# A decoder block's output projection: which heads it takes first, and where the attention's last pieces are put in place

## The chip, the cores and the metric

The kernel runs on one core of a Trainium2 chip. What counts is the device time of one execution in microseconds; the times below are medians of several executions. The core has a matrix engine (TensorE, PE in the profile, with PEld for its weight loads), a vector engine (VectorE, DVE), an activation engine (ScalarE, ACT), a general engine (GpSimd, POOL) and a queue engine (SyncE, SP), which here only issues DMAs. ACT and POOL also issue DMAs.

## The reference, cut to what matters

```python
def token_mixer(h, ...):                       # h: [1, 512, 2048]
    proj = h @ w_in
    ...
    o_a = gla_chunked(...)                     # linear attention, 4 heads of 256 columns
    gate = jax.nn.silu(gg)                     # gg: 1024 columns of proj
    o_a = (rmsnorm(o_a, gla_norm) * gate).reshape(B, S, GLA_V)
    ...
    o_b = diff_attention(dq, dk, dv, lam)      # softmax attention, 4 heads of 256 columns
    o_b = (rmsnorm(o_b, diff_norm) * (1.0 - lambda_init)).reshape(B, S, DIFF_V)
    o = jnp.concatenate([o_a, o_b], axis=-1)   # [1, 512, 2048]
    return o @ w_o                             # w_o: [2048, 2048]

x = x + rmsnorm(token_mixer(rmsnorm(x)), attn_post_norm)
x = x + rmsnorm(conv_ffn(rmsnorm(x)), ffn_post_norm)
```

Rows 0 to 1023 of `w_o` meet the linear attention's heads, rows 1024 to 2047 the softmax attention's. All is float32.

## The kernel before, in words

**Split products.** Every large product is done with each float32 operand split in two parts of a faster kind, `hi` and `lo`, and three matmuls (hi·hi, hi·lo, lo·hi). Activations stand in SBUF as `ah` and `al`, [128, 4 token blocks, 16 slots of 128 features, 128 tokens]. Weights come in tiles of 512 KB (`raw`, four buffers; `wt` for some) on the SP queue. `granule` (L128) splits one: ACT copies it to `hi` (L137), DVE subtracts to get `lo` (L138). The parts go to `ring`, which holds three tiles.

**Units.** The input projection is done mostly in ten units (`InUnit`, L696). A unit makes a 2 by 2 block product of tokens by columns with seven block products instead of eight, called x0, z0, y0, z1, x1, y1, y2. Each takes two weight tiles, 24 matmuls of 128x128 on 128x256 each (L742 to L748). The operands are `ah`/`al` itself or sums of its blocks: x0 reads block a11 (tokens 0 to 255, slots 0 to 7), x1 reads a12 (the same tokens, slots 8 to 15), y1 reads s7, which was written over tokens 256 to 511, slots 0 to 7, and y2 reads a22 (tokens 256 to 511, slots 8 to 15). y1 and y2 use weight tiles to which POOL's DMAs have added another block (`more`, L720). The last two units, `gate_unit(0)` and `gate_unit(1)`, make the gate of the linear attention. Each of their four results is multiplied with a head's output loaded from DRAM (`op`), passed through a sigmoid and multiplied again (L819 to L821). The first unit's results go to DRAM (`ogd`); the second's are kept in SBUF (`kept_u`).

**Attention beside them.** The two attentions are generators in the list `fill`, the linear one first. `step()` is called after each weight tile and moves them on by `pace[0]` steps, 0.75 for most of the projection; `drain()` runs what is left. The softmax attention (`diff_heads`, L586) has 16 pieces of work (4 heads by 4 query blocks) in a pipeline of 21 steps: scores and softmax, transposes two steps later (L637), the product with the values another step later (L646) with its square sum on ACT (L649), its root on POOL (L144, L146) and the scaling on DVE (L652), and two steps later the transposes of the result (L659), a copy (L661) and a store to DRAM from ACT (`dstd`, L662). Each step of the generator is program order for all engines.

**Putting in place.** Two helpers bring the mixer's result into `ah` and `al`, whose old contents the units have then done with. `place_diff(i)` does the softmax attention: for each head it loads tokens 256 i to 256 i + 255 from `dstd` (`dt`, 256 KB, on SP) and splits them into slots 0 to 7, on ACT (L150) and DVE (L151). `turn_gate(i)` does the gated linear attention for the same tokens: it loads `ogt` from `ogd` (256 KB, on SP), transposes that and the kept blocks on PE (L833) and splits them into slots 8 to 15 with the same two lines. `dt` and `ogt` share the four buffers of the tag `qk` with the attention's queries and keys.

**Output projection.** `proj_n` (L196) makes 512 columns at a time: for each weight tile (two slots of 128 rows) and each of four token blocks six matmuls of 128x128 on 128x512 (L191 to L193) into four PSUM banks. It takes three column blocks; the fourth is in `to_ffn`, which goes on into the next norm and the feed-forward part and whose order on the engines is written out by hand (`manual_schedule`). Before the change the weight rows come as 1024 to 2047, then 0 to 1023, against slots 0 to 15.

**What sets the order.** Outside the hand-ordered blocks a planner orders each engine's instructions at build time, by program order and by when its own timing model says that inputs and buffers are there. At run time each engine's queue keeps that order, and each instruction waits for its inputs.

The end of the mixer, for the last unit, reads before the change: `u.y0()`, `u.z1()`, `drain()`, `place_diff(0)`, `u.x1()`, `turn_gate(0)`, `u.y1()`, `place_diff(1)`, `u.y2()`, `turn_gate(1)`.

Of the kernel before, what the change touches and what calls it, by code (L numbers as in the profile page):

```python
# [21 lines left out]
KT = D // P  # L22
# [13 lines left out]
def hybrid_layer(ctx: ExitStack, tc: tile.TileContext, x, attn_pre_norm, w_in, w_alpha_up, b_alpha,  # L36
# [6 lines left out]
    w_o3 = w_o[0].rearrange("(k p) c -> p k c", p=P)  # L43
# [37 lines left out]
    pace = [0.0, 0.0]  # L81
# [13 lines left out]
    def drain():  # L95
        while fill:
            for _ in fill.pop(0):
                pass

    def load(src, a, by=None):  # L100
        raw = wpool.tile([P, GR], F32, name="raw", tag="raw", bufs=4)
        (by or nc.sync).dma_start(out=raw.rearrange("p (a b) -> p a b", a=a), in_=src)
        return raw
# [9 lines left out]
    def halves():  # L113
        slot[0] = (slot[0] + 1) % 3
        return [ring[:, RS * i + p:RS * i + p + GR] for i, p in zip((slot[0], slot[0] + 3), place_w[0])]
# [3 lines left out]
    def spare_halves(pool):  # L119
        if pool == "rt":  # L120
            return [rp.tile([P, GR], F32R, name=n, tag="rt", bufs=4) for n in ("xhi", "xlo")]
        if pool is True:
            if not kept:
                kept.extend(small_tile(n, F32R) for n in ("xhi", "xlo"))
            return kept
        return [pool.tile([P, GR], F32R, name=n, tag=n, bufs=4) for n in ("xhi", "xlo")]

    def granule(src, a, raw=None, spare=None, hl=None):  # L128
        if raw is None:
            raw = load(src, a)  # L130
        if hl is not None:
            hi, lo = hl[:, 0, :], hl[:, 1, :]
        elif spare:
            hi, lo = spare_halves(spare)
        else:
            hi, lo = halves()
        act(hi, raw, AF.Copy)  # L137
        tt(lo, raw, hi.bitcast(F32), ALU.subtract)  # L138
        r = "p (a b) -> p a b"
        return hi.rearrange(r, a=a), lo.rearrange(r, a=a)  # L140
# [43 lines left out]
                    emit(n, banks[n])  # L184
            step()

    def mm_n(banks, t, g, w):
        for k in range(2):
            s = 2 * g + k
            st, sp = s == 0, s == KT - 1  # L190
            mm(banks[t], ah[:, t, s, :], w[0][:, k, :], start=st, stop=False)  # L191
            mm(banks[t], ah[:, t, s, :], w[1][:, k, :], start=False, stop=False)  # L192
            mm(banks[t], al[:, t, s, :], w[0][:, k, :], start=False, stop=sp)  # L193


    def proj_n(w3, col, emit, order=tuple(range(KT)), first=0, banks=None):  # L196
        if banks is None:
            banks = [bank(psm) for _ in range(NT)]
        for g in range(first, KT // 2):
            w = granule(w3[:, order[2 * g]:order[2 * g] + 2, col:col + 512], 2)  # L200
            for t in range(NT):
                mm_n(banks, t, g, w)
                if g == KT // 2 - 1:
                    emit(t, banks[t])
            step()
# [96 lines left out]
    with tc.manual_schedule(engines=IN_ORDER):  # L302
        banks = first_half(0)

    HK = KT // 2
# [11 lines left out]
    sp = mixer.enter_context(tc.tile_pool(name="sums", bufs=1))  # L317
# [521 lines left out]
    def turn_gate(i):  # L839
        for j in range(2):  # L840
            u = qk_tile("ogt")
            dma(two(u), ogd[:, 2 * i:2 * i + 2, 256 * j:256 * (j + 1)])
            turn_block(0, j, i, u)
            turn_block(1, j, i, kept_u.pop((j, i)))

    def place_diff(i):
        for h in range(DH):
            u = qk_tile("dt")
            dma(two(u), dstd[h][:, :, 256 * i:256 * (i + 1)])
            split(*(v[:, 2 * i:2 * i + 2, 2 * h:2 * h + 2, :].rearrange("p t n c -> p n t c") for v in (ah, al)),  # L850
                  u.rearrange("p (n t c) -> p n t c", n=2, t=2))
# [41 lines left out]
    banks = [bank(psm) for _ in range(2)]  # L893
# [14 lines left out]
    for i, u in enumerate(units):  # L908
        u.y0()
        if i - 1 in after:  # L910
            there[after[i - 1][0]] = after[i - 1][1]
        u.z1()
        pace[0] = 0.75
        if i < len(units) - 1:
            u.x1()
            u.y1()
            units[i + 1].x0()
            u.y2()
            units[i + 1].z0()
        else:  # L920
            drain()
            place_diff(0)
            u.x1()
            turn_gate(0)
            u.y1()
            place_diff(1)
            u.y2()
            turn_gate(1)
    mixer.close()


    x1d = [dram.tile([P, D], F32, name=f"x1d{t}") for t in range(NT)]
    wo = ExitStack()
    wp = wo.enter_context(tc.tile_pool(name="wo", bufs=1))
    m = [wp.tile([P, D], F32, name=f"m{t}") for t in range(NT)]
    g1 = wp.tile([P, D], F32, name="g1")
    g2 = wp.tile([P, D], F32, name="g2")
# [4 lines left out]
    def evac_m(c, t, b):  # L942
        sl = slice(512 * c, 512 * (c + 1))
        act(m[t][:, sl], b, AF.Square, accum_out=ssm[t][:, c:c + 1])
        tt(m[t][:, sl], b, g1[:, sl], ALU.mult)

    order = [(s + 8) % 16 for s in range(KT)]
    for c in range(3):
        proj_n(w_o3, 512 * c, lambda t, b, c=c: evac_m(c, t, b), order)

    def to_ffn():
        banks = [bank(psm) for _ in range(NT)]
        w, wa, wb, xr, rs = {}, {}, {}, {}, {}

        def weights(g):
            w[g] = granule(w_o3[:, order[2 * g]:order[2 * g] + 2, 1536:2048], 2, spare=wp if g > 3 else None)

        def prods(t, *gs):  # L960
            for g in gs:
                mm_n(banks, t, g, w[g])

        def evac(t):
            xr[t] = wp.tile([P, D], F32, name="xr", tag="xr", bufs=2)
            dma(xr[t], x2[t * P:(t + 1) * P, :])
            evac_m(3, t, banks[t])
            ss = small.tile([P, 1], F32, name="ss", tag="ss")
            nc.vector.reduce_sum(ss, ssm[t], axis=AX.X)
            rs[t] = rsqrt_mean(ss, D)  # L970

        def residual(t):
            stt(m[t], m[t], rs[t], xr[t], ALU.mult, ALU.add)
            dma(x1d[t], m[t])

        def square(t):
            ss = small.tile([P, 1], F32, name="ss", tag="ss")
            act(xr[t], m[t], AF.Square, accum_out=ss)
            rs[t] = rsqrt_mean(ss, D)

        def scale(t):
            for i in range(4):
                sl = slice(512 * i, 512 * (i + 1))
                stt(xr[t][:, sl], m[t][:, sl], rs[t], g2[:, sl], ALU.mult, ALU.mult)

        def turn(t, *ps):
            for i in ps:
                transpose_into_act(xr[t][:, 512 * i:512 * (i + 1)], t, 4 * i, 4)

        def weights_f(d, c0, g, spare=None):  # L990
            place_w[0] = APART
            d[g] = granule(w_f3[:, 4 * g:4 * g + 4, c0:c0 + 256], 4, spare=spare)

        for g in (0, 1, 2, 4):
            weights(g)
        for t in range(NT):
            prods(t, 0)
        for g in (3, 5, 6, 7):
            weights(g)
        prods(0, 1, 2, 3, 4, 5, 6, 7)  # L1000
        evac(0)
        residual(0)
        square(0)
        scale(0)
        prods(1, 1, 2, 3, 4, 5, 6, 7)
        evac(1)
        turn(0, 0, 1)
        residual(1)
        turn(0, 2, 3)
        square(1)  # L1010
        scale(1)
        prods(2, 1, 2, 3, 4, 5, 6, 7)
        evac(2)
        turn(1, 0, 1)
        residual(2)
        turn(1, 2, 3)
        square(2)
        prods(3, 1, 2, 3, 4, 5, 6, 7)
        weights_f(wa, 0, 0)
        weights_f(wa, 0, 1)  # L1020
        scale(2)
        evac(3)
        weights_f(wa, 0, 2)
        ba = [bank(psm) for _ in range(2)]
        bb = [bank(psm) for _ in range(2)]
        mm_t(ba, 0, wa[0], 0, 2)
        residual(3)
        turn(2, 0, 1, 2, 3)
        square(3)
        weights_f(wa, 0, 3, wp)  # L1030
        mm_t(ba, 1, wa[1], 0, 2)
        mm_t(ba, 2, wa[2], 0, 2)
        scale(3)
        weights_f(wb, DFF, 0, wp)
        mm_t(ba, 3, wa[3], 0, 2)
        turn(3, 0, 1, 2, 3)
        weights_f(wb, DFF, 1, wp)
        weights_f(wb, DFF, 2, wp)
        for g in range(3):
            mm_t(bb, g, wb[g], 0, 2)  # L1040
        for g in range(4):
            mm_t(ba, g, wa[g], 2, 4)
        bb2 = [bank() for _ in range(2)]
        for g in range(3):
            mm_t(bb2, g, wb[g], 2, 4)
        weights_f(wb, DFF, 3)
        mm_t(bb, 3, wb[3], 0, 2)
        mm_t(bb2, 3, wb[3], 2, 4)
        return ba, list(zip(bb, bb2))
# [444 lines left out]
    order = change_over(ups[-1])  # L1494
# [9 lines left out]
    for i, u in enumerate(downs):  # L1504
# [4 lines left out]
        first = i % 2 == 0  # L1509
# [147 lines left out]
```

## Time and profile before

| what | us |
|---|---|
| median of 3 runs | 2103.01 |
| lowest and highest run | 2099.64, 2104.24 |
| the profiled execution, its span (first to last instruction) | 2104.4 |
| PE busy in that span | 2062.8 (98%) |
| DVE busy | 1507.9 (72%) |
| ACT busy | 1001.9 (48%) |
| POOL busy | 287.5 (14%) |
| mean granted clock of TensorE | 0.996 |

No time of the profiled execution is given beside its span. A busy PE is not PE at its best: matmuls are pipelined and the profile models their ends. In the rows below a line such as L659 is that line of the kernel, `bank<-ident,on` names what is written and read, and a bracket at the end says how long the engine was idle before and which instruction ended that. Times are from the start of the span.

### The profile page before, as it was taken

The numbers are of one execution on the slowest core, as the hardware profiler recorded it, in microseconds if no ns is written. First come the engines' busy times: TensorE is split into PE (matmuls) and PEld (weight loads), VectorE is DVE, ScalarE is ACT, GpSimd is POOL, SyncE is SP. The second block draws the span as 40 slices with busy tenths as digits, with TensorE's granted clock in tenths as the row PEclk, the third lists the DMA queues.
The fourth block names the chain that finished last, engine by engine and source line by source line (L and its number), as shares of the span: only waits on it lengthen the run. The fifth ranks groups of instructions, "written<-read, shape, count | busy, mean of one in ns | idle before, by whom it ended". The sixth has DMA issues, their size and how long they took to land.

```text
span 2104.4 us, 35571 instructions
## 1 busy us (share of the span) xinstructions
PE 2062.8 (98%) x14449; PEld 1903.4 (90%) x14449; DVE 1507.9 (72%) x1802; ACT 1001.9 (48%) x1306; POOL 287.5 (14%) x306
## 2 busy tenths in 40 slices
PE   7999999999989999999999999999999999999998
PEld 6699999999988889899999999999999878787786
DVE  5967777676752255986777767777777778888877
ACT  4544444455742233454554545455455554444443
POOL 0112222322200000011111011111111110110100
PEclk9999999999999999999999999999999999999999
DMA  5488887878875344447668577567676876776663
GB/s 210 118 185 179 191 197 176 178 176 198 196 193 175 100 150 161 140 103 196 150 147 196 140 162 190 135 163 175 164 160 179 239 208 168 192 189 159 171 169 140
DMA packets 280696, 358.60 MB, mean 170 GB/s; under 512 B 14592, under 2 KB 221876, under 8 KB 278612
## 3 DMA queue, kind: packets, MB, share of 16 engines
q1 hardware_dynamic: 191380, 259.85, 37.1%
q0 software_dynamic: 84800, 94.38, 29.6%
q8 instruction: 113, 1.85, 0.4%
q10 hardware_dynamic: 4352, 2.10, 0.3%
q14 instruction: 51, 0.42, 0.1%
HBM read 311.72 MB, written 44.56 MB: 169 GB/s over the span
## 4 chain that ended last, share of the span: by engine, by line
issue 37%; PE 29%; POOL 3%; DMA 2%; DVE 2%; ACT 1%; POOLq 0%; DVEq 0%; ACTq 0%; SPq 0%
PE bank L1248 4%; PE bank L1247 4%; PE bank L1246 4%; PE bank L191 3%; PE bank L192 3%; PE bank L193 3%; POOL raw L1194 1%; POOL rt L1194 1%; PE bank L1349 1%; PE bank L1350 1%; PE bank L1348 1%; PE bank L1553 1%; PE bank L1554 1%; PE bank L1552 1%; PE bank L175 1%
## 5 line engine op out<-in xcount | busy, mean ns | idle before, releaser
L138 DVE TENSOR_TENSOR ring<-raw,ring 128x1024 fp32r<-128x1024 f32 x315 | 383.1, 1221 | 280.8 <-ACT ring L137 276.5
L137 ACT ACTIVATE ring<-raw 128x1024 fp32r<-128x1024 f32 x315 | 333.3, 1060 | 516.4 <-PE bank L1247 119.7
L1248 PE MATMUL bank<-ah,ring 128*128 128x256 f32 x1280 | 353.4, 276 | 0.7 <-DVE ring L138 0.7
L1246 PE MATMUL bank<-ah,ring 128*128 128x256 f32 x1280 | 353.3, 276 | 0.0
L1247 PE MATMUL bank<-al,ring 128*128 128x256 f32 x1280 | 353.3, 276 | 0.0
L137 ACT ACTIVATE ring<-rt 128x1024 fp32r<-128x1024 f32 x221 | 233.2, 1060 | 247.3 <-PE bank L1247 146.1
L138 DVE TENSOR_TENSOR ring<-rt,ring 128x1024 fp32r<-128x1024 f32 x221 | 268.8, 1221 | 91.6 <-ACT ring L137 89.7
L1248 PEld LDWEIGHTS bank<-ah,ring 128*128 128x128 f32 x1280 | 240.3, 188 | 0.9 <-DVE ring L138 0.9
L1246 PEld LDWEIGHTS bank<-ah,ring 128*128 128x128 f32 x1280 | 240.3, 188 | 0.1
L1247 PEld LDWEIGHTS bank<-al,ring 128*128 128x128 f32 x1280 | 240.3, 188 | 0.1
L1349 PE MATMUL bank<-ring,ah 128*128 128x512 f32 x424 | 166.2, 392 | 6.3 <-DVE ring L138 6.3
L1350 PE MATMUL bank<-ring,al 128*128 128x512 f32 x424 | 165.1, 389 | 0.0
L1348 PE MATMUL bank<-ring,ah 128*128 128x512 f32 x424 | 158.6, 391 | 0.7 <-ACT ring L137 0.7
L192 PE MATMUL bank<-ring,ah 128*128 128x512 f32 x280 | 111.1, 398 | 0.8 <-DVE ring L138 0.8
L191 PE MATMUL bank<-ring,ah 128*128 128x512 f32 x280 | 110.5, 400 | 0.3 <-ACT ah L150 0.3
L193 PE MATMUL bank<-ring,al 128*128 128x512 f32 x280 | 110.0, 396 | 0.0
L1194 POOL DMA_DIRECT2D raw<-in_w_ffn_in_dram x40 | 51.2, 1309 | 397.2 <-DVE ring L138 397.2
L1349 PEld LDWEIGHTS bank<-ring,ah 128*128 128x128 f32 x424 | 79.6, 188 | 26.0 <-DVE ring L138 9.9
L1348 PEld LDWEIGHTS bank<-ring,ah 128*128 128x128 f32 x424 | 79.3, 188 | 19.8 <-ACT ring L137 3.2
L1194 POOL DMA_DIRECT2D rt<-in_w_ffn_in_dram x40 | 51.0, 1285 | 326.2 <-DVE ring L138 303.7
L1350 PEld LDWEIGHTS bank<-ring,al 128*128 128x128 f32 x424 | 79.6, 188 | 16.4
L746 PE MATMUL bank<-ring,ah 128*128 128x256 f32 x320 | 92.6, 289 | 0.0
(346 smaller groups left out, 5675.3 us busy)
## 6 DMA issues: line engine op xcount, KB each, us to landing
raw<-in_w_ffn_in_dram SPq DMA_DIRECT2D x96, 512.0 KB, 5.0
raw<-in_w_in_dram SPq DMA_DIRECT2D x56, 512.0 KB, 4.6
raw<-in_w_ffn_out_dram SPq DMA_DIRECT2D x48, 512.0 KB, 6.8
raw<-in_w_in_dram POOLq DMA_DIRECT2D x40, 512.0 KB, 7.2
rt<-in_w_ffn_in_dram SPq DMA_DIRECT2D x40, 512.0 KB, 5.9
rt<-in_w_ffn_in_dram POOLq DMA_DIRECT2D x40, 512.0 KB, 6.1
raw<-in_w_ffn_in_dram POOLq DMA_DIRECT2D x40, 512.0 KB, 6.8
raw<-in_w_o_dram SPq DMA_DIRECT2D x32, 512.0 KB, 3.9
```

Of the source, the lines that this page charges most:

```text
L137: act(hi, raw, AF.Copy)
L138: tt(lo, raw, hi.bitcast(F32), ALU.subtract)
L191: mm(banks[t], ah[:, t, s, :], w[0][:, k, :], start=st, stop=False)
L192: mm(banks[t], ah[:, t, s, :], w[1][:, k, :], start=False, stop=False)
L193: mm(banks[t], al[:, t, s, :], w[0][:, k, :], start=False, stop=sp)
L1194: nc.gpsimd.dma_start(out=raws[g].rearrange("p (a b) -> p a b", a=self.a), in_=self.block(0, j, g), accum_op=ALU.add)
L1246: mm(o, wh, sh[:, :, kk, :], start=start and kk == 0 and n == 0, stop=False, **NOW)
L1247: mm(o, wh, sl[:, :, kk, :], start=False, stop=False, **NOW)
L1248: mm(o, wl, sh[:, :, kk, :], start=False, stop=kk == HK - 1, **NOW)
L1348: mm(b[j], sh[:, o:o + P], w[0][:, q, :], start=start and st == 0, stop=False, **NOW)
L1349: mm(b[j], sh[:, o:o + P], w[1][:, q, :], start=False, stop=False, **NOW)
L1350: mm(b[j], sl[:, o:o + P], w[0][:, q, :], start=False, stop=st == 3, **NOW)
```

## The change

The linear attention's heads come first in the output projection: weight rows 0 to 1023 are taken first and meet slots 8 to 15. `proj_n` and `mm_n` get a list of slots in place of an order of weight rows. `place_diff(0)`, `place_diff(1)` and `drain()` move behind `turn_gate(1)`, and the pace for the last three block products is set to one attention step for each call. The pool of the output projection's tiles, which lies over the mixer's memory, is made with `reuse_waits="tile"`: each of its tiles waits only for what lay under it, not for the whole pool before it.

```diff
-    def mm_n(banks, t, g, w):
+    def mm_n(banks, t, g, w, slots=tuple(range(KT))):
         for k in range(2):
-            s = 2 * g + k
-            st, sp = s == 0, s == KT - 1
+            i = 2 * g + k
+            st, sp, s = i == 0, i == KT - 1, slots[i]
             mm(banks[t], ah[:, t, s, :], w[0][:, k, :], start=st, stop=False)
...
-    def proj_n(w3, col, emit, order=tuple(range(KT)), first=0, banks=None):
+    def proj_n(w3, col, emit, slots=tuple(range(KT)), first=0, banks=None):
...
-            w = granule(w3[:, order[2 * g]:order[2 * g] + 2, col:col + 512], 2)
+            w = granule(w3[:, 2 * g:2 * g + 2, col:col + 512], 2)
             for t in range(NT):
-                mm_n(banks, t, g, w)
+                mm_n(banks, t, g, w, slots)
...
         else:
-            drain()
-            place_diff(0)
+            pace[0] = 1.0
             u.x1()
             turn_gate(0)
             u.y1()
-            place_diff(1)
             u.y2()
             turn_gate(1)
+            drain()
+            place_diff(0)
+            place_diff(1)
     mixer.close()
...
-    wp = wo.enter_context(tc.tile_pool(name="wo", bufs=1))
+    wp = wo.enter_context(tc.tile_pool(name="wo", bufs=1, reuse_waits="tile"))
...
-    order = [(s + 8) % 16 for s in range(KT)]
+    slots = [(s + HK) % KT for s in range(KT)]
     for c in range(3):
-        proj_n(w_o3, 512 * c, lambda t, b, c=c: evac_m(c, t, b), order)
+        proj_n(w_o3, 512 * c, lambda t, b, c=c: evac_m(c, t, b), slots)
...
-            w[g] = granule(w_o3[:, order[2 * g]:order[2 * g] + 2, 1536:2048], 2, spare=wp if g > 3 else None)
+            w[g] = granule(w_o3[:, 2 * g:2 * g + 2, 1536:2048], 2, spare=wp if g > 3 else None)
...
-                mm_n(banks, t, g, w[g])
+                mm_n(banks, t, g, w[g], slots)
```

## The prediction

> **What bounds the kernel now.** I read the page's first part, then TensorE's busy time by stretches around the edit, then the stretch that stands out, engine by engine.
>
> ```profile
> span 2104.4 us, 35571 instructions
> ...
> PE 2062.8 (98%) x14449; PEld 1903.4 (90%) x14449; DVE 1507.9 (72%) x1802; ACT 1001.9 (48%) x1306; POOL 287.5 (14%) x306
> ```
>
> TensorE (PE) is busy for 98% of the span, so what moves the time is a hole on PE or a slower PE. All idle time together is 2104.4 - 2062.8 = 41.6 us, and what the edit can win lies in the part of it near the edit. By stretches (length, then busy time of PE, PEld, DVE, ACT, POOL, then granted clock, DMA share, GB/s):
>
> ```profile
> 540.00:550.00 10.00, 8.60 (x63) 7.98 (x62) 7.62 (x16) 7.46 (x15) 2.55 (x3) 1.00 0.76 217
> ...
> 580.00:590.00 10.00, 10.00 (x82) 9.79 (x81) 3.06 (x3) 3.09 (x4) 2.91 (x3) 1.00 1.20 221
> 590.00:600.00 10.00, 4.30 (x22) 4.13 (x22) 3.92 (x6) 3.87 (x8) 0.88 (x2) 0.76 1.10 344
> 600.00:610.00 10.00, 10.00 (x82) 10.00 (x82) 7.15 (x10) 5.64 (x8) 0.00 (x0) 0.90 0.55 165
> ...
> 630.00:640.00 10.00, 10.00 (x46) 8.28 (x45) 3.31 (x4) 2.12 (x2) 0.00 (x0) 1.00 0.99 372
> ```
>
> The stretch from 590 to 600 us has 22 matmuls where its neighbours have 82, and the clock falls to 0.76 and 0.90 in it and the next. That stretch is the last gate unit's z1 and x1, where the edit is. PE in order of time (start, length, instruction, idle time before it):
>
> ```profile
> 584.22 1.89 PE L646 MATMUL bank<-dvt,aT 128*128 128x256 f32 x8
> ...
> 590.07 0.28 PE L746 MATMUL bank<-ring,in_s3h 128*128 128x256 f32 x1
> 596.05 0.66 PE L659 MATMUL bank<-ident,on 128*128 128x128 f32 x2 [5.70 <-DVE on L652]
> ...
> 596.93 0.41 PE L746 MATMUL bank<-ring,in_s3h 128*128 128x256 f32 x1
> ...
> 601.63 0.41 PE L747 MATMUL bank<-ring,al 128*128 128x256 f32 x1
> ...
> 602.04 0.28 PE L746 MATMUL bank<-ring,ah 128*128 128x256 f32 x1
> 602.15 0.28 PE L747 MATMUL bank<-ring,al 128*128 128x256 f32 x1
> ```
>
> PE stands 5.70 us in front of the transposes of the last attention step's output (L659), in the middle of z1's products. The value product that feeds them (L646, four key blocks) began at 584.22 and is modelled to end at 586.1. Why the output came so late is on ScalarE (ACT):
>
> ```profile
> 593.34 0.63 ACT L150 ACTIVATE ah<-dt 128x512 fp32r<-128x512 f32 x1 [7.94 <-DMA dt<-dstd]
> 593.87 0.37 ACT L649 ACTIVATE jk<-bank 128x256 f32<-128x256 f32 x1
> ```
>
> ACT stood 7.94 us before the first half of a split of `dt`, the fourth of `place_diff(0)`, and the square of the last attention step (L649) was behind it. In the program that square comes before `place_diff`; the planner, which sets the order here, put it behind. The chain of waits says what the split waited for (start, length):
>
> ```profile
> 579.90 7.53 DMA dstd<-dst
> 587.48 5.83 DMA dt<-dstd
> ```
>
> A store of 128 KB to DRAM and its load back, 13.4 us, in the stretch where the DMA share is 1.20. So the chain is: store, reload, split on ACT, square, norm, transposes, with PE's z1 products queued behind the transposes.
>
> **The change, part by part.**
>
> *The drain and the pace.* `step()` is called twice in each block product. Counting calls from where the two generators start, with 0.75 of a step each, the 53 steps of the linear attention, and the attention's steps with their yields while a head is not there, step 18 falls on z0's second half of the last unit, step 19 on y0's first and step 20, the last, on y0's second; z1's second half finds the generator ended. So `drain()` had nothing to do, and `pace[0] = 1.0` paces nothing. Moving them costs and gains 0. The attention's instructions are issued where they were; "dealt out" does not happen.
>
> *`place_diff` behind everything.* Its 8 loads on the SP queue, 8 splits on ACT and 8 on DVE remain in number. In program order they move past x1, y1, y2 and both `turn_gate`s, and on SP past three `op` loads and four `ogt` loads. The SP queue now:
>
> ```profile
> 587.48 0.52 SPq L48 DMA_DIRECT2D dt<-dstd  x1
> 588.11 0.61 SPq L48 DMA_DIRECT2D op<-oad  x1
> 588.78 1.00 SPq L48 DMA_DIRECT2D ogt<-ogd  x2
> ...
> 591.59 0.38 SPq L102 DMA_DIRECT2D raw<-in_w_o_dram  x1
> ```
>
> The fourth `dt` held up `op`, `ogt` and the first weights of w_o behind it. With the move, `ogt` takes the four buffers of tag qk first, so no `dt` can be asked for before an `ogt` is transposed, after x1. ACT then has nothing to stand before when the last value product ends. From square to transposes took 596.05 - 593.87 = 2.2 us; from 586.1 that is 588.3, before PE comes to the place at 590.35. The wait of 5.70 us goes; for a slower norm or an earlier place of the transposes I leave 0.2 us.
>
> *The clock behind the hole.* From 596.93 to 601.63 lie 23 matmuls, 22 steps of 0.214 us, where 602.04 to 602.15 is 0.11 us: 22 x 0.10 = 2.2 us lost. The two clock figures say the same from the other side: half clock for 4.8 and 2.0 us, of which PE worked from 596.05 to 602.0; half of that is 3.0 us. I take 2.8 us, since the rows leave out the edges. [...] The rows of 540 to 550 show the other side: 1.4 us idle, clock 1.00. So a short hole costs only itself.
>
> *What comes late next.* PE reaches y1 and y2 8.5 us earlier. y1's weights are the slowest, added to in place by POOL's DMAs, and the loads that matter land so (median us last):
>
> ```profile
> raw<-in_w_o_dram SPq DMA_DIRECT2D x10, 512.0 KB, 4.2
> ...
> dt<-dstd SPq DMA_DIRECT2D x8, 256.0 KB, 6.4
> ...
> raw<-in_w_in_dram POOLq DMA_DIRECT2D x2, 512.0 KB, 9.5
> ```
>
> ```profile
> 583.07 1.27 POOL L720 DMA_DIRECT2D raw<-in_w_in_dram  x1 [0.91 <-DVE ring L138]
> ```
>
> 583.07 + 9.5 = 592.6. y1's second half starts on PE after 590.35, eight matmuls of z1, x1's 48 and y1's first 24, at 0.11 us each: at 599.2. Its tile must be split before, 2.3 us: 4 us to spare. Cost 0, bounds 0 to 2 us.
>
> *The projection's order.* Same weights, same matmuls; `slots` only pairs weight rows 0 to 7 with `ah`, `al` slots 8 to 15. At 46 matmuls per 10 us, the 96 that read slots 8 to 15 in the first column block take 20.9 us. They are the cover for `place_diff`: two rounds through four buffers at 6.4 us plus 1.3 us of split each, 15.4 us. So the move costs 0 while that cover stands; without it, a `dt` reload stands on PE's path. What is newly exposed is `turn_gate(1)`: its splits for tokens 256 to 511 may not write before y2's last product has read that place.
>
> ```profile
> 618.72 0.28 PE L748 MATMUL bank<-ring,ah 128*128 128x256 f32 x1
> ```
>
> ```profile
> 622.59 0.69 DVE L821 TENSOR_TENSOR u<-u,op 128x512 f32<-128x512 f32 x1
> ```
>
> From y2's last product (to 619.0) to its gated block was 4.3 us, plus transposes and split, some 2 us: 6.3 us. That block goes to slots 12 to 15, first read there after two weight tiles and half of the third, 60 matmuls or 13 us. The blocks from `ogt` are ready for transposing before, and need about 2 us against 2.6 us of products of tokens 0 to 255. Cost 0, bounds 0 to 3 us.
>
> *`reuse_waits="tile"`.* The two broadcast gains were loaded late:
>
> ```profile
> 629.38 0.34 SPq L48 DMA_DIRECT2D g<-in_attn_post_norm_dram  x1
> ```
>
> They may now go earlier: 2 MB, 5.6 us at the 372 GB/s of 630 to 640. The first w_o tile, asked for at 591.59, lands at 595.8; its product comes after y2, at 619.0 - 8.5 = 610.5. Even 5.6 us later it is there. Cost 0, bounds 0 to 1 us; nothing here shows a gain beyond the hole.
>
> **Sum.** 5.7 - 0.2 + 2.8 = 8.3 us: the profiled span would go from 2104.4 to 2096.1. The page gives this execution only as its span, 1.4 us above the median of the runs (2103.0). Taken from the median: 2094.7 us.
>
> **The rivals.**
>
> *Half a gain.* The wait goes, but at the hand-over to w_o a hole of 3 us opens, by the bounds above. [...] For it: ACT and DVE get the eight late splits in the same 20 us as eight splits of `turn_gate`. Against: 20.9 us of products and DVE idle two thirds from 630 to 640.
>
> *The hole belongs to the load on the DMA queues.* [...] The rows have 13.4 us at a DMA share of 1.20, and the rows decide. But in runs with less crowding the hole could be smaller; the lowest run is 3.4 us below the median, which a smaller hole could explain. If the usual hole is half: 2099 us.
>
> *The doing is in the planner's hands, and nothing changes.* Program order put the square before the split already, and the planner did otherwise. If it again finds a split ready by its own reckoning ahead of the square, the hole stays: 2103 us. Against: the buffers of qk are taken by `ogt` until x1 is done.
>
> *Slower.* The same wait moves in front of the weight splits. The place: a `dt` split on ACT, planned for when the model thinks the reload is there, with the next weight tiles' halves (L137) behind it during x1 to y2. The ring holds three tiles, so PE has two tiles of 24 matmuls ahead, 5.3 us, less the 2.3 us of making one: 3 us. A stand of 7.94 us leaves a hole of 4.9 us and 2.8 us of clock, 7.7 us. One such hole gives back the gain (2102.4); from the second on the kernel is slower: 2110 us. For it: there are two groups of reloads, one behind each pair of stores. Against: the stores are long done by then, so only the load's 6.4 us is left to misjudge.
>
> **How the numbers follow.** Likeliest case 0.60, half a gain 0.13, smaller hole 0.06, nothing 0.10, one hole on the slower side 0.02, two 0.09. What a replanned order does to the small holes further down I put at 3 us either way. The range is 2090 (the forecast, less 3 us and the runs' own scatter) to 2104, which leaves 0.09 above for the two holes and some 0.05 below. About 0.2%, 4.2 us, is what can be told from no change: below 2098.8 is faster. The likeliest case and 0.11 of half a gain lie there: 0.71. Slower is the two holes and 0.01 of "nothing": 0.10. The rest is the same: 0.19.
>
> **What would show it.** In the changed profile: no wait of microseconds before L659; L649 on ACT within a microsecond of the value product; clock 1.00 from 590 to 610; `ogt` ahead of `dt` on SP; the first L191 some 8 us earlier; no idle PE in the first 21 us of the projection. It is wrong if a `dt` split again has a square or a weight split behind it on ACT with microseconds of idleness, or if PE waits for `turn_gate(1)` after y2.

## The result and the profile after

| | runs | median us | lowest and highest us |
|---|---|---|---|
| before, beside it | 20 | 2104.35 | 2099.64, 2112.62 |
| after | 20 | 2101.47 | 2097.49, 2105.56 |

The ratio of after to before is 0.9983, with an interval of 0.9975 to 0.9991: 0.17% or 3.6 us faster (1.9 to 5.3); the two medians lie 2.9 us apart. A second set of runs (e6 below) gave 0.9994 (0.9985 to 1.0003). The time forecast was 2094.7 us with a gain of 8.3 us; the gain is less than half of that.

The profiled execution alone would have hidden this. The page's head:

```profile
span 2095.8 us, 35570 instructions
...
PE 2059.0 (98%) x14449; PEld 1900.7 (91%) x14449; DVE 1509.7 (72%) x1802; ACT 1002.5 (48%) x1306; POOL 286.3 (14%) x306
```

Its span is 8.6 us below that of before, close to the sum forecast, but by luck. This execution is the fastest of its twenty: its time is 2097.49 us, 1.7 us more than its span and 4.0 us below the median. With the same 1.7 us the profiled execution of before took an estimated 2106.1 us, 1.7 us above the median in the table. To see what the edit itself does I cut the span on PE into three: up to the last score product of the softmax attention (`dk,dq`), from there to the first transposes of the next norm (`ident,xr`), and the rest. PE in order of time, before and then after:

```profile
561.39 1.88 PE L614 MATMUL bank<-dk,dq 128*128 128x512 f32 x4
...
775.03 1.91 PE L158 MATMUL bank<-ident,xr 128*128 128x128 f32 x16
```

```profile
559.51 1.88 PE L614 MATMUL bank<-dk,dq 128*128 128x512 f32 x4
...
769.40 1.96 PE L158 MATMUL bank<-ident,xr 128*128 128x128 f32 x16
```

The middle part, called the stage from here on, holds the edit and takes 213.64 us before and 209.89 us after: 3.75 us. Of the 8.6 us of the spans, 1.88 us lie ahead of the edit and 3.0 us behind the stage. In the other executions shown below the first part ends between 558.3 and 561.8 us, and the last part takes 1325.1 to 1329.4 us in five executions (before twice, after twice, e10) and up to 1332.5 us in the others. So a span carries several us of scatter from places that the edit doesn't touch, and the stage is the fairer measure of one execution.

TensorE by stretches (columns as in the prediction):

```profile
540.00:550.00 10.00, 8.70 (x67) 8.19 (x65) 8.55 (x21) 8.32 (x18) 3.66 (x4) 1.00 0.78 211
...
580.00:590.00 10.00, 10.00 (x90) 10.00 (x89) 4.54 (x5) 4.57 (x8) 2.06 (x3) 1.00 1.09 232
590.00:600.00 10.00, 8.72 (x75) 8.32 (x73) 3.67 (x5) 3.50 (x5) 0.00 (x0) 1.00 0.88 231
600.00:610.00 10.00, 8.86 (x61) 8.65 (x62) 9.28 (x13) 6.17 (x11) 0.00 (x0) 0.83 0.43 133
610.00:620.00 10.00, 10.00 (x58) 8.83 (x58) 9.26 (x14) 7.38 (x12) 0.00 (x0) 1.00 0.71 226
```

The stretch with 22 matmuls is gone (90 and 75 now), but 600 to 610 has 61 where before had 82, with a clock of 0.83. Hole and slow clock have moved 10 us down, to y1, and become smaller. PE in order of time:

```profile
583.86 0.38 PE L659 MATMUL bank<-ident,on 128*128 128x128 f32 x2
...
599.19 0.39 PE L746 MATMUL bank<-ring,ah 128*128 128x256 f32 x1 [0.97 <-ACT ring L137]
600.45 0.38 PE L748 MATMUL bank<-ring,ah 128*128 128x256 f32 x1 [0.76 <-DVE ring L138]
...
603.95 0.41 PE L747 MATMUL bank<-ring,al 128*128 128x256 f32 x1
...
607.28 0.36 PE L746 MATMUL bank<-ring,ah 128*128 128x256 f32 x1 [0.69 <-ACT ah L150]
```

The transposes L659 no longer wait: 5.70 us gone. In their place stand 0.97, 0.76 and 0.69 us, together 2.42. The first two are the two parts of y1's second weight tile, the third is y2's first product. ACT says why:

```profile
579.88 0.38 ACT L649 ACTIVATE jk<-bank 128x256 f32<-128x256 f32 x1 [2.01 <-PE bank L646]
...
598.08 1.06 ACT L137 ACTIVATE ring<-raw 128x1024 fp32r<-128x1024 f32 x1 [4.28 <-DMA raw<-in_w_in_dram]
...
605.18 0.63 ACT L150 ACTIVATE ah<-dt 128x512 fp32r<-128x512 f32 x1 [1.85 <-DMA dt<-dstd]
```

The square L649 now runs when the value product ends, as forecast. The planner has also put that value product itself earlier, 18.4 us behind the start of the stage (577.90) where before it was 22.8 (584.22 - 561.39); the prediction had left the attention's instructions where they were. e8 below has it as early (577.51, stage from 559.10) and still loses the time, so this isn't where the gain comes from. The split of y1's second tile waits 4.28 us for its data, the tile that POOL's DMA adds to. When it was asked for, and how long it took (an answer for 583 to 584 us):

```profile
583.38 1.31 POOL L720 DMA_DIRECT2D raw<-in_w_in_dram  x1 [2.10 <-DVE ring L138]
```

```profile
raw<-in_w_in_dram POOLq DMA_DIRECT2D x1, 512.0 KB, 14.6
```

It was asked for 0.3 us later than before (583.07) and took 14.6 us, where the same transfer before took 9.9. What ran beside it is on the SP queue:

```profile
575.94 2.05 SPq L48 DMA_DIRECT2D op<-oad  x4
579.89 1.90 SPq L48 DMA_DIRECT2D ogt<-ogd  x2
586.17 14.62 SPq L102 DMA_DIRECT2D raw<-in_w_o_dram  x4
600.88 7.51 SPq L48 DMA_DIRECT2D dt<-dstd  x4
```

Before, the fourth `dt` held this queue until 587.48; `op` and `ogt` came behind it and the first w_o tile at 591.59. Now `op` is asked for from 575.9, `ogt` from 579.9, w_o from 586.2, all while the adding DMAs run.

### The profile page after: what moved, and what is told of

Its sections match the earlier page's. It is cut to its first block, busy times and chain, and to the rows that moved or that the text cites. A ratio compares the mean times of both kernels' runs of the same rounds, so it can differ in the third digit from the quotient of the medians.

```text
span 2095.8 us, 35570 instructions
## 1 busy us (share of the span) xinstructions
PE 2059.0 (98%) x14449; PEld 1900.7 (91%) x14449; DVE 1509.7 (72%) x1802; ACT 1002.5 (48%) x1306; POOL 286.3 (14%) x306
## 3 DMA queue, kind: packets, MB, share of 16 engines
q8 instruction: 113, 1.85, 0.4%
## 4 chain that ended last, share of the span: by engine, by line
PE 60%; issue 30%; DMA 3%; DVE 3%; POOL 3%; ACT 1%; SPq 0%; POOLq 0%; DVEq 0%; ACTq 0%
PE bank L1247 6%; PE bank L1248 6%; PE bank L1249 6%; PE bank L192 3%; PE bank L193 3%; PE bank L191 3%; PE bank L742 3%; PE bank L744 3%; PE bank L743 3%; PE bank L746 3%; PE bank L748 3%; PE bank L747 3%; PE bank L173 2%; PE bank L175 2%; PE bank L174 2%
## 5 line engine op out<-in xcount | busy, mean ns | idle before, releaser
L191 PE MATMUL bank<-ring,ah 128*128 128x512 f32 x280 | 109.6, 397 | 0.0
```

## The experiments

My theory after these rows: the change takes away the hole it was forecast to take away, worth some 8 us of the stage, and half of that comes back at y1 because a queue that is no longer held lets early loads slow the adding DMAs. Rivals: the old hole was an accident of one execution; the move does nothing and the new order of heads does; the late `dt` splits themselves cost the time.

In the table a gap is each idle time of PE of 0.2 us or more in the stage, landing is how long the last adding DMA (y1's second tile) took, and the ratio is to the runs of before beside it. The experiments ran on three chips (e1 to e4; e5 to e8; e9 and e10), so kernels of different groups are better compared by the stage than by their ratios.

| kernel | stage us | gaps us | landing us | ratio (interval) |
|---|---|---|---|---|
| before | 213.64 | 5.70 | 9.9 | |
| e5, before again | 212.66 | 5.36 | 9.6 | |
| e10, order of heads alone | 213.36 | 5.59 | 9.9 | 0.9993 (0.9980 to 1.0006) |
| e8, before, square first | 214.88 | 5.95, 0.46 | 9.3 | 1.0000 (0.9989 to 1.0011) |
| after | 209.89 | 0.97, 0.76, 0.69 | 14.6 | 0.9983 (0.9975 to 0.9991) |
| e6, after again | 209.14 | 0.33, 0.76, 0.88, 1.24 | 14.0 | 0.9994 (0.9985 to 1.0003) |
| e4, move alone | 210.18 | 1.37, 0.76, 0.52 | 15.2 | 0.9979 (0.9968 to 0.9989) |
| e1, after, plain add | 210.56 | 3.20, 0.23 | no such DMA | 0.9991 (0.9980 to 1.0002) |
| e2, after, splits late | 209.55 | 0.36, 0.76, 0.48, 0.76, 0.89 | 15.8 | 0.9980 (0.9969 to 0.9991) |
| e3, after, w_o loads late | 207.26 | 0.89, 0.46, 0.25 | 12.4 | 0.9969 (0.9956 to 0.9981) |
| e7, both late | 205.13 | none | 11.4 | 0.9973 (0.9960 to 0.9985) |
| e9, both late, softmax heads first | 212.52 | 0.88, 2.08, 1.16 | 12.4 | 0.9990 (0.9979 to 1.0001) |

### Was the hole there in every execution: before again (e5) and after again (e6), unedited

> The kernel before, unchanged, for a second profile. Theory: the hole before L659 is part of every execution, 5 to 6 us, with about 5 us of halved clock behind it, since what makes it is the order on ACT and a store and reload under the same four adding DMAs. Rival: it belongs to the crowding of one execution; the hole is then 3 us or less and the clock may stay up, which would by itself explain why the change gained half of what its profile promised.

Before has the hole again. PE in e5:

```profile
593.99 0.66 PE L659 MATMUL bank<-ident,on 128*128 128x128 f32 x2 [5.36 <-DVE on L652]
```

> The changed kernel, unchanged, for a second profile and five more rounds. Theory: y1's second tile lands 13 to 16 us after its issue again, PE stands 1 to 3 us at y1, and the time is 3 to 4 us under the kernel before, ratio 0.9983. Rival: the late tile was one execution's; PE does not stand at y1 and the ratio has another cause.

After again stands at y1's second tile and at y2's first product, and there is no wait at L659. PE and its stretch in e6:

```profile
600.89 0.39 PE L746 MATMUL bank<-ring,ah 128*128 128x256 f32 x1 [0.33 <-ACT ring L137]
602.15 0.39 PE L748 MATMUL bank<-ring,ah 128*128 128x256 f32 x1 [0.76 <-DVE ring L138]
```

```profile
600.00:610.00 10.00, 6.79 (x53) 5.98 (x53) 8.37 (x11) 6.93 (x11) 0.00 (x0) 1.00 0.30 94
```

Its landing of 14.0 us agrees with 14.6. The clock does not: it stays at 1.00 here. What e6 has instead are longer gaps further on, 0.88 us for a gated block and 1.24 us at y2. The spans of these two, 2097.0 (before) and 2098.3 us (after), stand the other way round from their stages, 212.66 and 209.14: one more warning against a single span.

### What made the hole: before, the square ahead of the reload (e8)

```diff
-            place_diff(0)
+            with tc.issue_after(last_square[0].ins):
+                place_diff(0)
```

(`last_square[0]` is the last L649; lines of this kernel are one higher.)

> The kernel before, with the splits of place_diff(0) queued on ACT behind the square of the last attention step, and nothing else. Theory: the wait of ACT is for the reload of dt, whoever stands behind it. The square runs at once, L659's hole goes, but ACT then stands the same 5 to 8 us in front of x1's weight splits, and PE with it, with the clock halved as before: the kernel's time stays within 2 us of before, ratio 0.999 to 1.001. Rival, as the prediction has it: only the square and what hangs on it matter, the hole is gone and nothing comes in its place: 8 us under the kernel before, ratio 0.996.

The hole at the transposes is gone and one of 5.95 us stands at x1. ACT in e8:

```profile
579.50 0.39 ACT L650 ACTIVATE jk<-bank 128x256 f32<-128x256 f32 x1 [2.07 <-PE bank L647]
...
593.23 0.63 ACT L150 ACTIVATE ah<-dt 128x512 fp32r<-128x512 f32 x1 [10.48 <-DMA dt<-dstd]
...
594.24 1.05 ACT L137 ACTIVATE ring<-raw 128x1024 fp32r<-128x1024 f32 x1
```

The square is free, but the weight split is now behind the same `dt` split. So the costly thing is the split on ACT that waits for a store and its reload, 7.94 us in before and 10.48 us here; what stands behind it in ACT's queue only decides where PE stops. This is also the mechanism of the prediction's slower rival, shown in another kernel.

### One part alone: the order of heads (e10) and the move (e4)

e10 is before with `slots` in place of `order`; e4 is before with only this:

```diff
-            drain()
-            place_diff(0)
...
-            place_diff(1)
...
             turn_gate(1)
+            place_diff(0)
+            place_diff(1)
```

e4 has no `drain()` at this place any more, and the pace stays at 0.75.

> The kernel before, with only the order of the heads changed in the projection; place_diff, drain and the pool's waits as before. Theory: the hole before L659, 5 to 6 us, and its halved clock stay, nothing stands in the projection in either order: ratio 0.999 to 1.001. Rival: with the linear heads first PE now stands for turn_gate(1)'s splits, which come last in this program order: slower by 2 to 4 us, ratio 1.001 to 1.002.

> The kernel before, with only place_diff(0) and place_diff(1) moved behind turn_gate(1); the projection still takes the softmax attention's heads first. Theory: the hole before L659 goes and the holes at y1 come, as in the changed kernel, and in addition the projection's first products now stand before the reloads of dt, with no cover: the first slots' tokens 256 to 511 are split some 3 us after y2, the last at about 624. So 2 to 4 us of PE waits at the projection's start: near the kernel before, ratio 0.998 to 1.000. Rival, the order of the heads does not matter since the planner puts the splits early enough: same as the changed kernel, 0.9983, with no PE wait in the projection.

The order alone keeps the hole (5.59 us) and the time. The move alone gives the stage of after within 0.3 to 1.0 us and a ratio as good; the waits that e4 was expected to have at the projection's start did not come. So the move does all of it, and in this form of the kernel the order of heads costs and brings nothing that can be told. The pace and the place of `drain()` need no run: e4 has neither, and the changed kernel with both as before is a program with the same instructions and waits in the same order on each engine.

### The new waits: the adding DMAs (e1), the splits (e2), the loads of w_o (e3)

e1 takes one adding DMA away: the block for y1's second tile comes by a plain load on SP and DVE adds it.

```diff
+                if self.by_hand and g == 1:
+                    v12 = mx.tile([P, GR], F32, name="v12", tag="v", bufs=1)
+                    dma(v12.rearrange("p (a b) -> p a b", a=4), self.block(i, j, g))
+                    tt(raws[g], raws[g], v12, ALU.add)
+                    continue
```

> The changed kernel, with one DMA exchanged: the second of the two weight tiles that POOL's DMA adds to in place for the last unit's y1 is instead loaded by an ordinary DMA into a free buffer and added on DVE (one more 1.2 us addition). Theory: in the changed kernel y1's second tile landed 14.6 us after its issue (583.4 to 598.0) where before it took 9.9, because SP, no longer held by a reload of dt, issues op, ogt and w_o loads beside the four adding DMAs; PE then stood 0.97 and 0.76 us, and the clock was halved for 3.4 us (1.7 us lost). Without that DMA all 3.4 us come back: 6 to 7 us under the kernel before, ratio about 0.9968; no idle PE at y1, clock 1.00 from 590 to 610. Rival A, the late tile belongs to that one execution and the usual loss lies elsewhere: no more than the changed kernel's gain, 0.9983. Rival B, the halved clock comes from the transposes, not from the holes: about 1.7 us of the 3.4 come back, 0.9975, and the clock still drops.

This did not isolate what it was made for. DVE in e1:

```profile
593.07 1.23 DVE L724 TENSOR_TENSOR raw<-raw,v 128x1024 f32<-128x1024 f32 x1 [7.19 <-DMA v<-in_w_in_dram]
594.22 1.22 DVE L138 TENSOR_TENSOR ring<-raw,ring 128x1024 fp32r<-128x1024 f32 x1
```

The added instruction was placed ahead of x1's weight split and waited 7.19 us for its load; PE then stood 3.20 us in x1. One wait was swapped for another of the same kind. PE does not stand at y1 in e1, but it also comes there later by this wait, so the run says nothing on the adding DMAs.

e2 and e3 each hold one group back. In e2 the splits of `dt` are issued after y2's last evacuation and the last gated block; in e3 the first column block's w_o loads are issued after the first `dt` load.

```diff
+            with tc.issue_after(u.end_act.ins), tc.issue_after(end_dve[0].ins):
+                place_diff(0)
+                place_diff(1)
```

```diff
+    with tc.issue_after(first_dt[0].ins):
+        proj_n(w_o3, 0, lambda t, b: evac_m(0, t, b), slots)
+    for c in range(1, 3):
```

> The changed kernel, with the eight splits of place_diff queued on ACT and DVE behind the last unit's y2 result. Theory: only the third hole goes, 0.69 us in front of y2's first product: y1's result (L787) stood on DVE behind the second half of a split of dt, which had waited for its reload. The two holes at y1 and the halved clock stay: 0.7 us under the changed kernel, ratio 0.9980 to 0.9983. Rival, the splits of dt on ACT and DVE are the main loss (they delay weight splits too): 3 to 4 us under the changed kernel, 0.9966. Other rival, the cover of 20.9 us is too short once the splits start only after y2: PE waits in the projection's second half, and the kernel is slower than the changed one.

> The changed kernel, with the first column block's w_o loads queued on SP behind the first load of dt, which waits for a buffer that comes free after x1. So no w_o load runs beside the adding DMAs; op and ogt loads still do. Theory, the part of it that blames the w_o loads (1 MB of them asked for before 590): y1's second tile lands 3 us or more earlier, the holes at y1 go and the clock stays up: 3.4 us under the changed kernel, ratio about 0.9968. Rival, the op and ogt loads (1.5 MB, 576 to 582) do the harm, or the four adding DMAs among themselves: the tile lands as late as before the edit, ratio 0.9983. Other rival, w_o's first tiles now come too late for the projection: slower than the changed kernel.

In e2 the wait for `ah L150` at y2's first product is gone, but the waits at y1 are there as before, now at both of its tiles, with a landing of 15.8 us: the reloads and their splits do not make y1 late. In e3 the SP queue and ACT read:

```profile
581.00 1.93 SPq L48 DMA_DIRECT2D ogt<-ogd  x2
596.55 0.57 SPq L48 DMA_DIRECT2D dt<-dstd  x1
597.24 2.38 SPq L102 DMA_DIRECT2D raw<-in_w_o_dram  x4
```

```profile
596.90 1.06 ACT L137 ACTIVATE ring<-raw 128x1024 fp32r<-128x1024 f32 x1 [2.32 <-DMA raw<-in_w_in_dram]
```

With w_o asked for 11 us later, the last adding DMA lands in 12.4 us, ACT waits 2.32 us and PE does not stand at y1 at all. What is left there is 0.46 us at y2's first product, behind a `dt` split on ACT and DVE, and 0.89 us for a gated block. The table says the same seven times: with w_o's loads early the last adding DMA lands in 14.0 to 15.8 us (after, e6, e4, e2), with them late in 11.4 to 12.4 us (e3, e7, e9), and PE stands at y1 in each of the first four and in none of the last three. So w_o's four loads are what made y1 late. That e3 is faster than its neighbours is read from its stage: by the runs its lead on e4 and e2, 1 to 2 us of median on the same chip, is within the intervals. `op` and `ogt`, early in e3 too, are candidates for the rest (12.4 against 9.3 to 9.9 us); neither was moved alone. In e8 `op` is early and `ogt` late, and the DMA lands in 9.3 us, which speaks for `ogt` as far as one execution can.

### Both, and both with the old order of heads (e7, e9)

e7 has the edits of e2 and e3; e9 is e7 with weight rows 1024 to 2047 and slots 0 to 7 first, as before.

> The changed kernel with both orders: the first w_o loads behind the first load of dt on SP, and the splits of dt behind y2's result on ACT and DVE. Theory: the holes at y1 go, the clock stays at 1.00, and the 0.5 us before y2, where y1's result stood on DVE behind a split of dt, goes too: 6.5 to 7 us under the kernel before, ratio 0.9966, as a version that beats both. Rival: with the splits behind y2 the projection's second half waits for them, and it is slower than with the loads moved alone (0.9969).

TensorE by stretches in e7:

```profile
590.00:600.00 10.00, 10.00 (x90) 9.95 (x88) 7.34 (x11) 5.66 (x7) 0.00 (x0) 1.00 0.74 170
600.00:610.00 10.00, 10.00 (x78) 9.36 (x76) 9.05 (x13) 7.08 (x11) 0.00 (x0) 1.00 0.77 261
610.00:620.00 10.00, 10.00 (x52) 8.42 (x51) 5.34 (x8) 4.47 (x9) 0.00 (x0) 1.00 0.49 166
```

No gap and full clock through the whole stage: 205.13 us, 8.5 us below before's. Its median, 2096.09 us against 2102.43 of before beside it, makes it faster than both kernels. After, run on the same chip beside it (e6), had 2100.71 us: 4.6 us more. The ratio gives 5.7 us against before, somewhat less than expected, and does not tell e7 from e3 (0.9973 and 0.9969); the 2.1 us between these two stand in the stage alone.

> The fastest version so far (w_o's loads behind the first load of dt, splits of dt behind y2), but with the projection taking the softmax attention's heads first, as before. Theory: the 20.9 us of products on the linear attention's heads are the cover for the late splits; there the splits ran from 609.1 to 623.5, the projection from 607.5. Without the cover PE stands 4 to 8 us at the projection's start, with 1.5 to 3 us of halved clock: 6 to 10 us slower than that version, ratio to the kernel before 0.9995 to 1.002. Rival: the planner asks for the reloads early enough and the order of the heads is worth nothing, as in the kernel with only the move: 0.9973.

PE in e9:

```profile
611.70 0.50 PE L191 MATMUL bank<-ring,ah 128*128 128x512 f32 x1 [2.08 <-ACT ah L150]
614.08 1.09 PE L837 MATMUL bank<-ident,u 128*128 128x128 f32 x4 [1.16 <-DVE u L824]
```

With the softmax heads first, the projection's products wait for the late splits, the clock from 610 to 620 falls to 0.66, and the stage is 7.4 us longer. The ratios, from different chips, differ by 3.6 us (0.9990 and 0.9973). So the order of heads, worth nothing beside the move as made, is what allows the splits to be late.

## Why the prediction was wrong by half

**The hole and its price: right.** e7's stage has neither hole nor slow clock. Against it before lost 8.51 us, of which the hole was 5.70, so 2.8 are left for the clock: the terms as forecast. In e5 the same sum is 7.53 = 5.36 + 2.2, in e10 8.23 = 5.59 + 2.6. These clock terms are what is left over; read by half microseconds, the clock is halved from 595.2 to 602.0 in before, from 590.7 to 597.5 in e5 and from 592.2 to 599.1 in e10. PE works in 6.0, 3.5 and 4.8 us of that, so half of it, 3.0, 1.8 and 2.4 us, is lost. The clock's term depends on where the hole falls, and 7.5 to 8.5 us were there to be won. The rivals "the hole belongs to the load" and "nothing changes" are refuted by e5, e10 and after.

**Drain, pace, order of heads, cover: right.** e4 and e10 show the order at nothing, the stretches from 610 on show no idle PE at the projection's start, and e9 shows what the cover is worth when splits are late: 7.4 us of the stage. `reuse_waits` alone was not run; e4 gains as much without it, and with it or without it each engine has the same order of instructions and only waits differ.

**"What comes late next": the step that failed.** It asked the right question of the right tile. It took 9.5 us to landing from a stretch in which the SP queue was held by the very `dt` load that the change moves. The section on SP counted what the queue would be free of, and not what the freed loads do to the DMAs beside them. With 14.6 us in place of 9.5 the tile lands at 598.0, not at 592.6, and after the split of 2.3 us PE has it from 599.2 to 600.4, where it was needed at some 598.2: the 4 us to spare became 1.7 us of waiting, within the bound of 2 us. The last adding DMA took 9.3 to 15.8 us in these kernels. The step from 11.4-12.4 to 14.0-15.8 us is the w_o loads'; what takes the time up to 9.3 us, no run shows.

**"A short hole costs only itself": failed too, in some executions.** That step was to keep the bound at 2 us. PE in after, by short stretches:

```profile
600.00:602.00 2.00, 1.55 (x8) 1.55 (x9) 1.97 (x4) 0.81 (x3) 0.00 (x0) 0.71 0.13 20
602.00:604.00 2.00, 2.00 (x12) 2.00 (x11) 2.00 (x4) 1.33 (x2) 0.00 (x0) 0.50 0.91 301
604.00:606.00 2.00, 2.00 (x19) 2.00 (x19) 1.35 (x3) 0.82 (x2) 0.00 (x0) 0.94 0.21 72
```

The clock was halved for 1.16 + 2 + 0.24 = 3.4 us, from two holes of 0.97 and 0.76 us with half a microsecond of work between them, and PE worked nearly all of it: 1.7 us lost. The step rested on one hole of 1.4 us in one execution; that two smaller ones close together can do it was not considered. e4 shows the same (1.37 and 0.76 us, 3.4 us of halved clock), e6 does not (0.33 and 0.76 us, clock 1.00). The rival "half a gain" has a hole of 3 us and counts most of its chance (0.11 of 0.13) below 2098.8 us, so it prices the hole at little more than its own length, 2094.7 + 3 = 2097.7 us. In no run's stage does the clock stay at 1.00 behind such a hole: behind e1's of 3.20 us it was halved for 3.4 us.

**The late splits on ACT and DVE: the slower rival in small.** 0.69 us in after, 1.24 in e6, in front of y2's first product, whose bank DVE reads (L787) behind a `dt` split. PE's row in after names ACT's L150, but L787 ends just before PE goes on (606.46 + 0.68 = 607.14, PE at 607.28); e3's row names L787 itself. e2 and e7 are without it.

**The sum as it came out.** After's stage lies 4.76 us above e7's: 2.42 of gaps, 1.7 of clock, 0.6 that no row names. 8.51 - 4.76 = 3.75 us, and 3.6 us by the runs. In e6 it is 4.01 us: 3.21 of gaps, no clock, 0.8 that no row names. So what comes late behind the move costs 4 to 5 us both times, and the clock is a part of that only in after. The rival "half a gain" had this size, but from a hole at the hand-over to w_o, where nothing stands.

**What the prediction said would show it.** No wait at L659, the square within 0.1 us of the value product's end (579.79), `ogt` ahead of `dt`: all there. Clock 1.00 from 590 to 610: not there. The first L191 8 us earlier: a poor sign, since before had one among y2's products at 612.6; y2's last product came at 612.9 where it was 618.7. Of the signs of being wrong one was there: at 605.18 ACT stood 1.85 us before a `dt` split that had a weight split behind it.

What stays open: the second set's ratio (0.9994) is nearer to no change than the first's, and the two intervals overlap only from 0.9985 to 0.9991. The stages of before, e5, after and e6 say the gain is 2.8 to 4.5 us, whichever two are compared; that is as much as the scatter of the runs outside the stage.

## What to carry to other kernels

When a load that waits is moved, read the queue behind it: here what it held started earlier (`ogt` at 579.9 us in place of 588.8, w_o at 586.2 in place of 591.6), and the landing time measured while it was held, 9.9 us, became 14.6 us. Put loads that are not needed for 20 us behind the ones that PE is about to use, as e3 does (landing 12.4 us), and put work that waits for a reload behind the last work that others wait for, as e7 does. Then check the cover (e9), and judge by the stage and by many runs: here the spans of one pair of profiles showed more than twice the gain there was.

## What the hardware showed unexpectedly

In these runs the clock was halved after far less idleness than the 5.70 us hole, too (0.97 + 0.76 us in after), and size alone does not tell when. Some 45 us ahead of the edit every kernel has one hole in front of L646. PE there in e5 and in e6:

```profile
544.59 1.56 PE L646 MATMUL bank<-dvt,aT 128*128 128x256 f32 x6 [1.96 <-ACT aT L639]
```

```profile
545.40 1.95 PE L646 MATMUL bank<-dvt,aT 128*128 128x256 f32 x6 [1.98 <-ACT aT L639]
```

Stretches of TensorE from 540 us, e5 and then e6:

```profile
540.00:552.00 12.00, 10.04 (x71) 9.35 (x70) 10.02 (x28) 10.22 (x23) 4.58 (x6) 1.00 0.86 211
```

```profile
540.00:552.00 12.00, 9.85 (x60) 8.70 (x59) 9.25 (x26) 9.53 (x22) 4.58 (x6) 0.86 0.84 208
```

1.96 us left the clock alone, 1.98 us (with 0.17 us some 2 us earlier) halved it for 0.14 of 12 us, doubled: 3.4 us again. In the other ten profiles this hole is 0.88 to 1.98 us long (1.98 in e8) and the clock stays at 1.00. In after 0.97 + 0.76 us was enough, in e2 0.36 + 0.76 us and then 0.48 + 0.76 us was not. In the rows read here the halved stretch has one of two lengths, whatever the hole: 3.4 us in after, e1, e4 and e6, 6.8 us in before, e5, e8, e10 and e9. What decides besides the size, no run shows. So in this kernel a hole of 1 to 2 us carries a risk of an estimated 1.7 us more (half of the 3.4 measured), and the prediction should have priced it so.

A store of 128 KB to DRAM took 7.53 us ahead of its reload before, and 8.88 us in e8 (the chain of waits):

```profile
577.46 8.88 DMA dstd<-dst
...
586.35 6.85 DMA dt<-dstd
```

15.7 us for the pair, 13.4 before. An instruction that waits for such a pair should stand behind work that is worth that much.
